# Making the sparse heads' masks beside the dilated heads instead of behind the threshold search

## The chip, the core and the metric

The kernel runs on one core of one Trainium2 chip. The core has five engines with a queue of instructions each, executed in order: TensorE (PE; its weight loads are shown apart as PEld), VectorE (DVE), ScalarE (ACT), GpSimd (POOL) and SyncE (SP), which issues the DMA transfers. The metric is the device time of one execution in microseconds (us).

## The reference

The reference is a decoder trunk of two layers on a sequence of 1024 tokens of 1024 numbers, all in float32. Each layer normalises x, projects it (`w_in`), runs 16 attention heads of three kinds, adds their output projection to x, and then runs a gated MLP with a short convolution. The three kinds of heads are:

- 4 MLA heads: causal attention with low-rank queries and keys;
- 8 dilated heads: the mixture of three dilated windows (1, 4 and 16), which the kernel computes as one attention with an additive mask `dil`;
- 4 sparse heads (DSA): an indexer scores every pair of query and key, and each query attends only its 256 best keys.

```
score = einsum(relu(q_idx . k_idx), w_idx)          # per query t and key s
score = where(s <= t, score, -inf)
_, sel = top_k(score, 256)                          # ties: the lower index wins
s = (q . k[sel]) * HEAD_DIM ** -0.5;  p = softmax(s);  o = p @ v[sel]
```

The kernel does not gather. For every query it finds the 256th best score (the threshold), and turns the score tile into an additive mask that is 0 for chosen keys and huge for the others.

## The kernel before, in words

Queries are cut into 8 blocks of 128, one per partition. The scores of block i, (i+1)*128 columns wide, lie in the tile `sc2` to `sc7`; blocks 0 and 1 have at most 256 keys and need no choice.

**The indexer** (`indexer`, L292 to L430) is a Python generator: it emits a few instructions, yields, and its caller emits other work in between. It makes the scores (up to L344), and then searches the thresholds bit by bit (L379 to L393): 32 rounds, in which VectorE counts for blocks 4, 5 and 6 (L365) and ScalarE for blocks 7, 3 and 2 (L384). **The masks** come last (L400 to L430). `select(i)` makes one: ScalarE takes the Sign of score minus threshold into a work tile (L405); VectorE marks the ties (L406), numbers them with a prefix sum (L407), works out how many ties are needed (L409, L410), and writes the mask over the score tile (L411, L412). Blocks 4, 5 and 6 come first. Then three steps count and look up the exact threshold of blocks 7, 3 and 2 (L417 to L426: count, mask off, minimum), L427 and L428 correct it, and these three blocks are selected. That is 15 yields: 6 for three blocks, 3 for the thresholds, 6 for three blocks. The work tiles have the tag `tk`, two slots of 4 KB.

**The order of the layer** (`layer`): the first projection (index queries and keys), the MLA projection with the MLA tiles, then six groups of 384 columns of the input projection (L745 to L769; matmul L285, eviction L754 and L756 into `zst`, from there by DMA to DRAM). Beside each tile of these the indexer is advanced by 6 yields (`step`, L760), and the MLA heads by 4 pieces. The weights of a column group lie in four tiles of the ring `w0` or `w1` (even or odd group), so the last group's lie in `w1`.

**The 12 dilated and sparse heads** (heads 4 to 11 dilated, 12 to 15 sparse; L828 to L844) follow as a software pipeline: in round h, the scores of head h+1 (`attn_scores`), the values of head h (`attn_values`) and the preparation of head h+2 (`attn_prep`) are woven together by `prop`, which advances each generator in proportion to its weight. The scores of a head take, for each block i, a matmul pair (L539), VectorE's evacuation with the mask and a running minimum (L541, 12 of them per head, tiles `pt0` to `pt7`), ScalarE's exponential (L545), a reciprocal (L547) and GpSimd's scaling (L549). The values take transposes of pt (L564), ScalarE's copy ph (L567), VectorE's remainder pl (L568) and matmuls (L572 to L575). Preparation is split on GpSimd (L203, L204, L522, L523), transposed (L501, L511) and copied by ScalarE (L502, L512). The mask of a sparse head is `sc[i]` (L808).

The tile framework gives each instruction a priority from its place in the program, raised by `high_priority`, and a scheduler lays down the order on each engine. So the order on an engine is not the program's, and the projection's last matmuls stand between the first heads' work.

**Memory** is laid out by hand. `LAY1` (projection stage) has `w1` at 80 to 104 KB and `tk` at 104 to 112; `LAY2` (heads 4 to 15) has head 5's `QA1` and `QB1` at 104 to 112, and nothing at 78 to 93.5. A tile waits for what last used its space.

Of the kernel before, what the change touches and what calls it, by code (L numbers as in the profile page):

```python
# [8 lines left out]
F32 = mybir.dt.float32  # L9
# [6 lines left out]
ALU = mybir.AluOpType  # L16

DEPTH = 2
S = 1024
D = 1024  # L20
P = 128
# [4 lines left out]
NEG = -3.0e38  # L26
TOPK = 256
# [10 lines left out]
PTS = [[(f"pt{i}{e}", 1, (i + 1) / 2) for i in range(8)] for e in range(2)]  # L38
# [5 lines left out]
LAYM = [(0, ("QA0", 1, 4), ("QB0", 1, 4), ("KS0", 1, 4), ("otmp", 1, 2), PTS[0][0], PTS[0][1], PTS[0][2], PTS[0][3], ("caus", 1, 4),  # L44
        ("VS", 1, 4), PTS[0][4], PTS[0][5], PTS[0][6], PTS[0][7], ("ph", 2, 2), ("pl", 2, 2), ("mix", 2, 2), ("KL", 1, 4))]
LAY2 = [(0, ("QA0", 1, 4), ("QB0", 1, 4), ("KS0", 1, 4), ("kx", 1, 4), ("qx", 1, 4), ("dil", 1, 4), ("VS", 2, 4), ("ph", 3, 2),
        ("pl", 3, 2), ("otmp", 1, 2), PTS[1][0], PTS[1][1], PTS[1][2], PTS[1][3], ("mix", 2, 2)), (56, PTS[0][7], PTS[0][1],
        PTS[0][2], PTS[0][3], PTS[0][4], PTS[0][6], PTS[0][0], ("KS1", 1, 4), PTS[0][5]), (93.5, PTS[1][5], PTS[1][6], PTS[1][7],
        ("QA1", 1, 4), ("QB1", 1, 4), ("VS", 1, 4), PTS[1][4], ("caus", 1, 1))]
at2 = lambda tag, *places: [(o, (tag, 1, 2)) for o in places]  # L50
# [89 lines left out]
class Trunk:  # L140
# [151 lines left out]
    def indexer(self, zi, sc, pool, causal_diag):  # L292

        nc = self.nc
# [31 lines left out]
        for h in range(8):  # L326
            qi, qn = qn, qprep(h + 1) if h < 7 else None
            yield
            for i in range(2, NT):
                wd = (i + 1) * P  # L330
# [20 lines left out]
        va, ve = ACT_TK, tuple(i for i in range(2, NT) if i not in ACT_TK)  # L351
# [5 lines left out]
        cv, ca, fa, na_ = cc[:, :nv], cc[:, nv:], ff[:, nv:], nn[:, nv:]  # L357
# [6 lines left out]
        def count(src, junk, out, thr, op):  # L364
            nc.vector.tensor_scalar(junk, src, thr, None, op0=op, op1=ALU.add, accum_out=out)  # L365

        cut, o, pack = {}, 2048, None
        for i in (*ve, None):
            wd = (i + 1) * P if i else (max(ve) + 1) * P
# [8 lines left out]
        for bit in range(31, -1, -1):  # L378
            w = -1.0 if bit == 31 else float(1 << bit)  # L379
            nxt = 1 << (bit - 1) if bit else 0  # L380
            for c in range(max(na, nv)):
                if c < na:
                    junk = self.main.tile([P, S], I8, name="junka", tag="junka", bufs=1)
                    nc.scalar.activation(junk[:, :(va[c] + 1) * P], sc[va[c]], AF.Sign, bias=ca[:, c:c + 1].bitcast(F32),  # L384
                                         accum_out=na_[:, c:c + 1])
# [9 lines left out]
        thr = {i: cv[:, c:c + 1].bitcast(F32) for c, i in enumerate(ve)}  # L395

        need, up = st("need", NT, F32), st("up", na, F32)
        nt_ = self.small.tile([P, NT, 8], F32, name="nt", tag="wi", bufs=1)[:, 0]

        def select(i):  # L400
            wd = (i + 1) * P
            sg, e = (pool.tile([P, S], F32, name="tk", tag="tk") for _ in range(2))
            sg, e, nd = sg[:, :wd], e[:, :wd], need[:, i:i + 1]
            nc.vector.tensor_scalar(nt_[:, i:i + 1], thr[i], -1.0, None, op0=ALU.mult)
            nc.scalar.activation(sg, sc[i], AF.Sign, bias=nt_[:, i:i + 1], accum_out=nd)  # L405
            nc.vector.tensor_scalar(e, sg, 0.0, None, op0=ALU.is_equal)  # L406
            nc.vector.tensor_tensor_scan(e, self.one.to_broadcast([P, wd]), e, 0.0, op0=ALU.mult, op1=ALU.add)  # L407
            yield
            nc.vector.tensor_scalar(nd, nd, -0.5, TOPK - wd / 2, op0=ALU.mult, op1=ALU.add)  # L409
            nc.vector.scalar_tensor_tensor(nd, e[:, wd - 1:wd], 0.5, nd, op0=ALU.mult, op1=ALU.add)  # L410
            nc.vector.scalar_tensor_tensor(e, e, nd, sg, op0=ALU.is_gt, op1=ALU.subtract)  # L411
            nc.vector.tensor_scalar(sc[i], e, 0.0, -NEG, op0=ALU.is_gt, op1=ALU.mult)  # L412
            yield

        for i in ve:
            yield from select(i)
        for c, i in enumerate(va):  # L417
            wd = (i + 1) * P
            t_ = ca[:, c:c + 1].bitcast(F32)
            b = pool.tile([P, S], F32, name="tk", tag="tk")  # L420
            count(sc[i], b[:, :wd], na_[:, c:c + 1], t_, ALU.is_gt)
            nc.vector.tensor_scalar(b[:, :wd], sc[i], t_, -NEG, op0=ALU.is_le, op1=ALU.mult)
            nc.vector.tensor_tensor_reduce(b[:, :wd], b[:, :wd], sc[i], op0=ALU.add, op1=ALU.min, scale=1.0,
                                           scalar=-NEG, accum_out=up[:, c:c + 1])
            thr[i] = t_
            yield  # L426
        nc.vector.tensor_scalar(fa, na_, float(TOPK), None, op0=ALU.is_ge)  # L427
        nc.vector.copy_predicated(ca.bitcast(F32), fa, up)  # L428
        for i in va:
            yield from select(i)  # L430

    def mla_tile(self, t, ps, kpe, up, pool, outs):

# [153 lines left out]
    def layer(self, l, hT):  # L587
        nc, tc, a = self.nc, self.tc, self.a
# [9 lines left out]
        sc = {i: scv.tile([P, (i + 1) * P], F32, tag=f"sc{i}") for i in range(2, NT)}  # L598
        pool = View(tc, 56, LAYS[0][0], *LAY1)
# [94 lines left out]
        def prop(*gens):  # L694

            st = [[0.0, 1.0 / m, g_] for m, g_ in gens]
            while st:
                e = min(st, key=lambda e_: e_[0] + e_[1] / 2)
                if next(e[2], 0) == 0:
                    st.remove(e)  # L700
                else:
                    yield
                e[0] += e[1]
# [18 lines left out]
        def fin(kb, mix):  # L722
            kg, kk = divmod(kb, 4)
            for g in range(2):
                hi = self.hT_tile(mixh, g, kg, 0)[:, kk]
                lo = self.hT_tile(mixh, g, kg, 1)[:, kk]
                self.split(hi, lo, mix[g], FE[g], "pool")
# [51 lines left out]
        pool = View(tc, 80, LAYS[0][0], *LAY2)  # L779
# [37 lines left out]
        def chain(*items):  # L817
            items = [i for i in items if i]
            def gen():
                for i in items:  # L820
                    yield from i[1]
            return (sum(i[0] for i in items), gen()) if items else None

        SC = lambda h, g: (4, self.attn_scores(heads[h], g, pool)) if h < n else None
        VA = lambda h, g: (4 * g + 5, self.attn_values(heads[h], g, pool)) if 0 <= h < n else None
        PR = lambda h: chain((5, self.attn_prep(heads[h], pool)), (1, self.attn_prep_v(heads[h], pool))) if h < n else None

        def go(*items):  # L828
            for _ in prop(*[i for i in items if i]):
                pass  # L830
        with tc.high_priority(HP2):
            go(PR(4))
            go(chain(SC(4, 0), SC(4, 1)), PR(5))
        for h in range(4, n):
            if h == SW:
                self.banks(**B2)
            if h in FIN:
                kb = FIN.index(h)
                z = self.main.tile([P, 2, 512], F32, name="zm", tag="raw", bufs=3)
                nc.sync.dma_start(z, mD[:, kb])  # L840
                fin(kb, (z[:, 0], z[:, 1]))
            with tc.high_priority(HP2 if h <= HPH else 0):
                go(chain(SC(h + 1, 0), SC(h + 1, 1)), chain(VA(h, 0), VA(h, 1)), PR(h + 2))
        pool.close()  # L844
        scv.close()
        return mixh
# [369 lines left out]
```

## Time and profile before

| | |
|---|---|
| median of the runs shown (3) | 2788.01 us (2786.67 to 2792.11) |
| the profiled execution's own time | 2787.77 us |
| its span, first to last instruction | 2786.0 us |
| mean granted TensorE clock | 0.991 of full speed |
| TensorE busy | 2671.8 us (96%) |
| VectorE busy | 2265.9 us (81%) |

The profile's page gives the busy time of each engine, the costliest groups of instructions by line and the chain of work that ended last; the trace behind it answers by window, line or tile. A matmul's end is modelled, so a busy TensorE is not necessarily at its peak. Layer 0 lies in the first half of the span, layer 1 in the second, with the same stages.

### The profile page before, as it was taken

What the parts mean: (1) busy time and instruction counts of PE and PEld (TensorE: products, weight loads), DVE (VectorE), ACT (ScalarE), POOL (GpSimd) and SP (SyncE); (2) the same over time, 40 slices, a digit from 0 to 9 for tenths busy, and PEclk for the clock granted to TensorE, in tenths of its full rate; (3) what the DMA queues carried; (4) which work ended last, traced back from release to release, by engine and by line L of the source; (5) the groups of instructions that cost most, each with busy time, mean ns of one, the idle gap of its engine ahead of it and who ended that gap; (6) DMA issues with size and microseconds to landing.
All of it is one profiled execution on the core that took longest, in us unless ns stands there. A gap on an engine that the chain in (4) does not pass through costs nothing.

```text
span 2786.0 us, 40647 instructions
## 1 busy us (share of the span) xinstructions
PE 2671.8 (96%) x13576; PEld 2264.1 (81%) x13576; DVE 2265.9 (81%) x4347; ACT 1564.8 (56%) x3414; POOL 1728.5 (62%) x1910
## 2 busy tenths in 40 slices
PE   7999999999899999999999999999998999999997
PEld 7898988878787787777789989888787777877775
DVE  7779996874788888889867799788648888888887
ACT  4567857982444454454445778489624444444443
POOL 5364467971576677777534445689517677767764
PEclk9999999999999999999999999999999999999999
DMA  5322323341111111211333223233501111111111
GB/s 166 101 90 87 101 82 90 99 132 45 38 46 51 52 50 50 63 55 46 99 100 108 88 77 108 85 95 92 160 9 38 54 46 54 60 49 51 54 53 76
DMA packets 224013, 208.85 MB, mean 75 GB/s; under 512 B 21852, under 2 KB 197820, under 8 KB 223804
## 3 DMA queue, kind: packets, MB, share of 16 engines
q1 hardware_dynamic: 223804, 206.26, 24.5%
q8 instruction: 107, 1.75, 0.3%
q14 instruction: 102, 0.84, 0.1%
HBM read 153.80 MB, written 39.85 MB: 70 GB/s over the span
## 4 chain that ended last, share of the span: by engine, by line
PE 68%; DVE 15%; POOL 6%; issue 5%; ACT 4%; DMA 3%; SPq 0%; POOLq 0%; ACTq 0%; DVEq 0%
PE psum L969 23%; PE psum L285 11%; PE psum L1071 10%; PE psum L934 6%; PE psum L539 4%; PE psum L564 4%; DVE cut L365 2%; DVE psum L1030 2%; DVE x L1075 2%; PE psum L575 2%; PE psum L574 1%; PE psum L572 1%; PE psum L1127 1%; POOL wu L204 1%; PE psum L335 1%
## 5 line engine op out<-in xcount | busy, mean ns | idle before, releaser
L204 POOL TENSOR_TENSOR wu<-raw,wu 128x256 fp32r<-128x256 f32 x584 | 480.2, 841 | 316.5 <-ACT wu L199 311.7
L285 PE MATMUL psum<-wi,hT 128*128 128x384 f32 (+1 forms) x3072 | 603.1, 339 | 0.9 <-ACT zst L756 0.9
L285 PEld LDWEIGHTS psum<-wi,hT 128*128 128x128 f32 x3072 | 528.8, 190 | 10.9 <-ACT zst L756 1.3
L969 PE MATMUL psum<-hT,wu 128*128 128x512 f32 x1824 | 491.2, 400 | 19.0 <-ACT wu L199 10.0
L1071 PE MATMUL psum<-wd,act 128*128 128x512 f32 x1680 | 470.3, 396 | 21.1 <-DVE x L1075 12.4
L199 ACT ACTIVATE wu<-raw 128x256 fp32r<-128x256 f32 x584 | 232.0, 415 | 439.8 <-PE psum L969 300.2
L1075 DVE TENSOR_TENSOR x<-psum,x 128x512 f32<-128x512 f32 x640 | 419.0, 682 | 37.2 <-PE psum L1071 36.7
L969 PEld LDWEIGHTS psum<-hT,wu 128*128 128x128 f32 x1824 | 346.1, 190 | 106.5 <-ACT wu L199 11.7
L1071 PEld LDWEIGHTS psum<-wd,act 128*128 128x128 f32 x1680 | 313.4, 188 | 107.1 <-DVE x L1075 22.4
L969 PE MATMUL psum<-T,wu 128*128 128x512 f32 x1440 | 380.7, 395 | 2.5 <-ACT act L199 1.3
L969 PEld LDWEIGHTS psum<-T,wu 128*128 128x128 f32 x1440 | 268.9, 188 | 70.5 <-POOL wu L204 3.3
L549 POOL TENSOR_SCALAR pt<-pt,rl 128x128 f32<-128x128 f32 (+7 forms) x256 | 192.0, 765 | 133.6 <-DVE rl L547 103.0
L568 DVE TENSOR_TENSOR pl<-psum,ph 128x512 fp32r<-128x512 f32 (+3 forms) x384 | 206.2, 552 | 37.7 <-ACT ph L567 35.6
L545 ACT ACTIVATE pt<-pt,nm 128x128 f32<-128x128 f32 (+7 forms) x256 | 198.7, 777 | 47.2 <-DVE nm L541 45.0
L204 POOL TENSOR_TENSOR act<-yu,act 128x512 fp32r<-128x512 f32 x140 | 195.9, 1399 | 43.4 <-ACT act L199 41.7
L204 POOL TENSOR_TENSOR wd<-wr,wd 128x512 fp32r<-128x512 f32 x140 | 197.5, 1411 | 9.0 <-ACT wd L199 8.6
L564 PE MATMUL psum<-ident,pt 128*128 128x128 f32 x1152 | 193.1, 276 | 9.6 <-DVE QB L514 4.5
L192 POOL TENSOR_TENSOR rs<-ms,mhalf 128x1 f32<-128x1 f32 (+1 forms) x56 | 37.5, 670 | 252.1 <-DVE ms L189 249.4
L567 ACT ACTIVATE ph<-psum 128x512 fp32r<-128x512 f32 (+3 forms) x384 | 179.0, 487 | 22.5 <-PE psum L564 17.5
L934 PE MATMUL psum<-wo,hT 128*128 128x512 f32 x768 | 190.5, 404 | 0.0
L384 ACT ACTIVATE junka<-sc,cc 128x1024 int8<-128x1024 f32 (+2 forms) x192 | 158.5, 825 | 40.1 <-DVE cc L393 32.1
L564 PEld LDWEIGHTS psum<-ident,pt 128*128 128x128 f32 x1152 | 141.1, 141 | 39.9 <-POOL pt L549 7.5
(234 smaller groups left out, 5309.6 us busy)
## 6 DMA issues: line engine op xcount, KB each, us to landing
raw<-in_w_up_dram SPq DMA_DIRECT2D x88, 512.0 KB, 4.0
raw<-in_w_in_dram SPq DMA_DIRECT2D x56, 384.0 KB, 3.4
wr<-in_w_down_dram SPq DMA_DIRECT2D x40, 512.0 KB, 3.3
z<-zst SPq DMA_DIRECT2D x96, 192.0 KB, 1.9
z<-z SPq DMA_DIRECT2D x36, 512.0 KB, 4.6
QB<-KS SPq DMA_DIRECT2D x96, 128.0 KB, 2.3
x<-in_x_dram SPq DMA_DIRECT2D x16, 512.0 KB, 5.1
raw<-in_w_o_dram SPq DMA_DIRECT2D x16, 512.0 KB, 3.4
```

The source lines that it names most:

```text
L199: nc.scalar.activation(hi, src, AF.Copy)
L204: (nc.vector if le == "dve" else nc.gpsimd).tensor_tensor(lo, src, r32(hi), op=ALU.subtract)
L285: mm = nc.tensor.matmul(ps[:, :w], l_, r_, start=(n == 0), stop=(n == 3 * KD - 1))
L545: nc.scalar.activation(pt, pt, AF.Exp, bias=nm, scale=-1.0, accum_out=ls[:, i % 2:i % 2 + 1])
L549: nc.gpsimd.tensor_scalar(p_, p_, rl[:, e:e + 1], 0.0, op0=ALU.mult, op1=ALU.add)
L564: nc.tensor.transpose(ps[:, (i - 4 * g) * P:(i - 4 * g + 1) * P], Pt[i][:, j * P:(j + 1) * P], self.ident)
L567: nc.scalar.activation(ph[:, off:], ps[:, off:], AF.Copy)
L568: nc.vector.tensor_tensor(pl[:, off:], ps[:, off:], r32(ph[:, off:]), op=ALU.subtract)
L934: nc.tensor.matmul(ps, l_, r_, start=(i == 0), stop=(i == 3 * KD - 1))
L969: nc.tensor.matmul(ps, l_, r_, start=(start and i == 0), stop=(stop and i == 11), skip_group_check=resume)
L1071: nc.tensor.matmul(ps, l_[:, a_, t * P:(t + 1) * P], r_[:, b_], start=(start and i == 0), stop=i == 2, skip_group_check=not start)
L1075: nc.vector.tensor_tensor(xs, ps, xs, op=ALU.add)
```

## The change

The masks' part of the indexer becomes a generator of its own, `masks(pool)`, which the indexer only defines. The layer starts it with the pool of the head stage, where two `tk` slots are added at 81 to 89 KB, and weaves it into rounds 4 to 8 of the heads, three yields in each: 5 x 3 = 15, all of it. What each instruction computes is unchanged.

```
-LAY2 = [(0, ...), (56, PTS[0][7], PTS[0][1],
+LAY2 = [(0, ...), (81, ("tk", 2, 4)), (56, PTS[0][7], PTS[0][1],
...
-        def select(i):
+        def select(i, pool):
...
-        for i in ve:
-            yield from select(i)
-        for c, i in enumerate(va):
...
-        for i in va:
-            yield from select(i)
+        def masks(pool):
+            for i in ve:
+                yield from select(i, pool)
+            for c, i in enumerate(va):
...
+            for i in va:
+                yield from select(i, pool)
+
+        self.masks = masks
...
+        masks = self.masks(pool)
+
+        def part(gen, m):
+            for _ in range(m):
+                next(gen, None)
+                yield
...
-                go(chain(SC(h + 1, 0), SC(h + 1, 1)), chain(VA(h, 0), VA(h, 1)), PR(h + 2))
+                go(chain(SC(h + 1, 0), SC(h + 1, 1)), chain(VA(h, 0), VA(h, 1)), PR(h + 2),
+                   (3, part(masks, 3)) if 4 <= h < 9 else None)
```

Lines behind L414 are renumbered in the kernel after: by 4 in the rest of the indexer and in the heads' functions (L541 becomes L545, L568 becomes L572), by 12 behind the heads' loop.

On VectorE, right behind the last round of the search in layer 0, the masks of blocks 4 and 5 (score tiles `sc_119` and `sc_120`) follow in the kernel before:

```order
L404 TENSOR_SCALAR nt<-cc 128x1
L568 TENSOR_TENSOR pl<-psum,ph 128x128
L409 TENSOR_SCALAR need<-need 128x1
L406 TENSOR_SCALAR tk<-tk 128x640
L407 SCALAR_TENSOR_TENSOR tk<-one,tk 128x640
L410 SCALAR_TENSOR_TENSOR need<-tk,need 128x1
L411 SCALAR_TENSOR_TENSOR tk<-tk,need 128x640
L412 TENSOR_SCALAR sc_119<-tk 128x640
L582 TENSOR_TENSOR mix<-psum,otmp 64x512
L409 TENSOR_SCALAR need<-need 128x1
L406 TENSOR_SCALAR tk<-tk 128x768
```

At the same place in the kernel after, the first scores of head 4 stand (L545 is the old L541; `pt_5055` and the next are its first key rows):

```order
L404 TENSOR_SCALAR nt<-cc 128x1 x3
L394 TENSOR_SCALAR cc<-cc 128x3
L572 TENSOR_TENSOR pl<-psum,ph 128x128
L586 TENSOR_TENSOR mix<-psum,otmp 64x512
L545 ISA pt_5055,nm<-psum,dil 128x128
L545 ISA nm 128x1
L545 ISA pt_5072,nm<-psum,dil 128x256
```

Nothing of the masks but the negated thresholds is left there. The second place on VectorE is head 5's fifth key row (`pt_5375` before, `pt_5317` after), which follows the projection's last matmuls. Before:

```order
L568 TENSOR_TENSOR pl<-psum,ph 128x384
L568 TENSOR_TENSOR pl<-psum,ph 128x256
L568 TENSOR_TENSOR pl<-psum,ph 128x128
L541 ISA pt_5375,nm<-psum,dil 128x512
L541 ISA nm 128x1
L541 ISA pt_5375,nm<-psum,dil,nm 128x128
L541 ISA nm 128x1
L541 ISA pt_5414,nm<-psum,dil 128x512
```

After, with what each instruction waits for besides its own engine's order:

```order
L406 TENSOR_SCALAR tk<-tk 128x640 [waits PE_49]
L572 TENSOR_TENSOR pl<-psum,ph 128x512 [waits Activation_49]
L407 SCALAR_TENSOR_TENSOR tk<-one,tk 128x640 [waits DVE_49]
L572 TENSOR_TENSOR pl<-psum,ph 128x384 [waits PE_49,Activation_49]
L410 SCALAR_TENSOR_TENSOR need<-tk,need 128x1 [waits DVE_49]
L411 SCALAR_TENSOR_TENSOR tk<-tk,need 128x640 [waits DVE_49]
L572 TENSOR_TENSOR pl<-psum,ph 128x512 [waits Activation_49]
L412 TENSOR_SCALAR sc_119<-tk 128x640 [waits DVE_49]
L545 ISA pt_5317,nm<-psum,dil 128x512 [waits DMAHW4_49,DMAHW2_49,DMAHW5_49,DMAHW1_49,DMAHW7_49,DMAHW0_49,Pool_49]
L545 ISA nm 128x1
L409 TENSOR_SCALAR need<-need 128x1 [waits Activation_49]
L406 TENSOR_SCALAR tk<-tk 128x768 [waits DVE_49]
```

The masks have moved in between the heads' evacuations and remainders, from here to head 9's seventh key row in layer 0 and to just behind head 10's first in layer 1, and their first step waits for TensorE. On ScalarE the Signs have moved with them. Here the first two of them are seen among the evacuations ph (L571, the old L567) of the values and head 5's exponential (L549, the old L545):

```order
L405 ACTIVATE tk,need<-sc_119,nt 128x640 [waits PE_49]
L571 ACTIVATE ph<-psum 128x512 [waits DVE_49,PE_49] x2
L760 ACTIVATE zst<-psum 128x384 [waits DMAHW0_49,PE_49,Pool_49]
L571 ACTIVATE ph<-psum 128x384 [waits DVE_49,PE_49]
L571 ACTIVATE ph<-psum 128x512 [waits PE_49]
L516 ACTIVATE QA<-psum 128x512 [waits DVE_49,PE_49]
L405 ACTIVATE tk,need<-sc_120,nt 128x768 [waits DVE_49]
L571 ACTIVATE ph<-psum 128x128 [waits DVE_49,PE_49]
L571 ACTIVATE ph<-psum 128x256 [waits PE_49]
L549 ACTIVATE pt_5317,ls<-pt_5317,nm 128x640 [waits DMAHW0_49,DMAHW7_49,DVE_49,Pool_49]
```

The second Sign waits for VectorE, since the two work slots are shared by all masks.

More of the change, by code (lines that the diff above doesn't have):

```diff
@@ L46 @@
 LAY2 = [(0, ("QA0", 1, 4), ("QB0", 1, 4), ("KS0", 1, 4), ("kx", 1, 4), ("qx", 1, 4), ("dil", 1, 4), ("VS", 2, 4), ("ph", 3, 2),
-        ("pl", 3, 2), ("otmp", 1, 2), PTS[1][0], PTS[1][1], PTS[1][2], PTS[1][3], ("mix", 2, 2)), (56, PTS[0][7], PTS[0][1],
+        ("pl", 3, 2), ("otmp", 1, 2), PTS[1][0], PTS[1][1], PTS[1][2], PTS[1][3], ("mix", 2, 2)), (81, ("tk", 2, 4)), (56, PTS[0][7], PTS[0][1],
         PTS[0][2], PTS[0][3], PTS[0][4], PTS[0][6], PTS[0][0], ("KS1", 1, 4), PTS[0][5]), (93.5, PTS[1][5], PTS[1][6], PTS[1][7],
@@ L413, in select @@
             yield
-        for i in ve:
-            yield from select(i)
-        for c, i in enumerate(va):
[L418 to L428, printed above, removed]
-        for i in va:
-            yield from select(i)
+        def masks(pool):
+            for i in ve:
+                yield from select(i, pool)
+            for c, i in enumerate(va):
+                wd = (i + 1) * P
+                t_ = ca[:, c:c + 1].bitcast(F32)
+                b = pool.tile([P, S], F32, name="tk", tag="tk")
+                count(sc[i], b[:, :wd], na_[:, c:c + 1], t_, ALU.is_gt)
+                nc.vector.tensor_scalar(b[:, :wd], sc[i], t_, -NEG, op0=ALU.is_le, op1=ALU.mult)
+                nc.vector.tensor_tensor_reduce(b[:, :wd], b[:, :wd], sc[i], op0=ALU.add, op1=ALU.min, scale=1.0,
+                                               scalar=-NEG, accum_out=up[:, c:c + 1])
+                thr[i] = t_
+                yield
+            nc.vector.tensor_scalar(fa, na_, float(TOPK), None, op0=ALU.is_ge)
+            nc.vector.copy_predicated(ca.bitcast(F32), fa, up)
+            for i in va:
+                yield from select(i, pool)
+        self.masks = masks
     def mla_tile(self, t, ps, kpe, up, pool, outs):
@@ L826, in layer @@
         PR = lambda h: chain((5, self.attn_prep(heads[h], pool)), (1, self.attn_prep_v(heads[h], pool))) if h < n else None
+        masks = self.masks(pool)
+        def part(gen, m):
+            for _ in range(m):
+                next(gen, None)
+                yield
         def go(*items):
```

## Prediction

> **What bounds the kernel now.** I read the page first, then cut the two layers into stretches with the table of windows, then looked up the masks in the groups by line, and last the order of time around them. The page says that TensorE is the busiest engine over the whole run, so a stretch in which it works without a break cannot be shortened by moving VectorE's work.
>
> ```profile
> span 2786.0 us, 40647 instructions
> PE 2671.8 (96%) x13576; PEld 2264.1 (81%) x13576; DVE 2265.9 (81%) x4347; ACT 1564.8 (56%) x3414; POOL 1728.5 (62%) x1910
> ```
>
> The shares are means over stages with different limits. Four instants cut layer 0: the search for the thresholds ends at about 374 us, the last matmul of the input projection (L285) starts at 437.55, head 5 makes its fifth key row (L541, pt4) at 444.88, and head 9 makes its seventh (pt6, counted as the 69th score evacuation of the dilated heads) at 503.30.
>
> ```profile
> 437.55 0.42 PE L285 MATMUL psum<-wi,hT 128*128 128x384 f32 x1
> ...
> 444.88 0.69 DVE L541 CUSTOM_DVE_ANT_0 pt<-psum,dil 128x512 f32<-128x512 f32 x1 [2.32 <-DMA z<-zst]
> ...
> 503.30 0.68 DVE L541 CUSTOM_DVE_ANT_0 pt<-psum,dil 128x512 f32<-128x512 f32 x1
> ```
>
> The windows between them (columns: length, then busy time and instructions of PE, weight load, DVE, ACT, POOL, then granted clock and DMA):
>
> ```profile
> core 0: us, PE busy (x) PEld busy (x) DVE busy (x) ACT busy (x) POOL busy (x), PEclk, DMA share, GB/s
> 374.00:437.60 63.60, 57.69 (x351) 53.81 (x349) 49.32 (x112) 28.84 (x67) 39.62 (x61) 1.00 0.31 90
> 437.60:444.90 7.30, 5.57 (x37) 4.43 (x35) 2.79 (x7) 4.00 (x9) 7.05 (x12) 1.00 0.51 135
> 444.90:503.30 58.40, 56.72 (x365) 48.01 (x366) 49.75 (x162) 53.02 (x127) 48.55 (x59) 0.97 0.35 92
> 503.30:624.00 120.70, 117.25 (x766) 99.73 (x766) 101.11 (x287) 107.59 (x246) 102.59 (x114) 0.99 0.40 114
> ```
>
> Two different regimes stand here. In the first window the projection's matmuls fill TensorE, which is busy 57.69 of 63.60 us, and the masks run on VectorE beside them: TensorE loses at most 63.60 - 57.69 = 5.9 us, whatever causes it. In the third window every engine is nearly full: VectorE 49.75 of 58.40 us (85%), ScalarE 91%, GpSimd 83%, TensorE 97%. VectorE has 58.40 - 49.75 = 8.65 us to spare there. This is where the change puts the masks.
>
> Layer 1 has the same shape. Its windows are cut at the same instructions, except that its last mask falls later in the new order, behind head 10's first row, so the third window ends there:
>
> ```profile
> 1754.00:1815.70 61.70, 57.14 (x340) 53.96 (x339) 46.59 (x97) 27.39 (x64) 44.31 (x64) 0.97 0.33 95
> 1820.20:1885.30 65.10, 64.55 (x437) 55.55 (x436) 58.36 (x183) 60.93 (x145) 56.52 (x69) 1.00 0.32 84
> 1885.30:1997.60 112.30, 109.23 (x719) 93.19 (x719) 92.70 (x270) 100.44 (x231) 96.00 (x107) 1.00 0.42 119
> ```
>
> **What is moved, and what it costs.** The groups of VectorE between 373 and 420 us hold the whole of layer 0's masks; the eight costliest of them (columns: count, busy us and mean ns, then idle time ahead) are these.
>
> ```profile
> L407 DVE TENSOR_TENSOR_SCAN tk<-one,tk 128x640 f32<-128x640 f32 (+5 forms) x6 | 10.9, 1811 | 0.1
> L411 DVE SCALAR_TENSOR_TENSOR tk<-tk,need 128x640 f32<-128x640 f32 (+5 forms) x6 | 6.2, 1041 | 0.2
> L412 DVE TENSOR_SCALAR sc<-tk 128x640 f32<-128x640 f32 (+5 forms) x6 | 4.9, 820 | 0.1
> L406 DVE TENSOR_SCALAR tk<-tk 128x640 f32<-128x640 f32 (+5 forms) x6 | 3.8, 625 | 0.1
> L423 DVE CUSTOM_DVE_ANT_0 tk<-tk,sc 128x1024 f32<-128x1024 f32 (+2 forms) x3 | 2.9, 979 | 0.0
> L422 DVE TENSOR_SCALAR tk<-sc,cc 128x1024 f32<-128x1024 f32 (+2 forms) x3 | 2.6, 881 | 0.0
> L365 DVE TENSOR_SCALAR_CACHE_REDUCE tk<-sc,cc 128x1024 f32<-128x1024 f32 (+2 forms) x3 | 2.6, 871 | 0.0
> L410 DVE SCALAR_TENSOR_TENSOR need<-tk,need 128x1 f32<-128x1 f32 x6 | 2.0, 328 | 0.2
> ```
>
> They sum to 35.9 us in a layer. The rest of the step is six Signs on ScalarE (L405) and a few very short instructions; no DMA, no matmul and nothing on GpSimd belongs to it, so no DMA queue is moved past anything. No instruction is added or taken away: the total work stays, and only its place counts.
>
> Term 1, the head start. With the masks gone from the first window, the heads' short chains no longer queue behind them, and TensorE can close its idle time there: between 0 and 5.9 us in layer 0, and 61.70 - 57.14 = 4.6 us in layer 1. About as many TensorE instructions stand ahead of the last projection matmul in the new order as in the old (a difference of some ten in 2400), so the projection's end comes earlier by that idle time and by no more. I take all of it, -5.9 and -4.6, because what TensorE waits for there is late GpSimd and VectorE work.
>
> Term 2, the first tile. The masks now need two work slots that lie in the projection's weight ring, so their first VectorE step waits for the projection's end, and so do the parts pl of head 4's values, which stand behind it in VectorE's queue and for which TensorE waits. That falls into the 7.30 us of the second window, where VectorE is busy for 2.79 and waits for the write of a `zst` tile (2.32 us in the row at 444.88), because head 5's pt4 takes over that space. The tile of 640 columns costs there what it costs now:
>
> ```profile
> 375.46 0.48 DVE L406 TENSOR_SCALAR tk<-tk 128x640 f32<-128x640 f32 x1
> 375.98 1.78 DVE L407 TENSOR_TENSOR_SCAN tk<-one,tk 128x640 f32<-128x640 f32 x1
> 377.79 1.07 DVE L410 SCALAR_TENSOR_TENSOR need<-tk,need 128x1 f32<-128x1 f32 x1
> 378.90 0.88 DVE L411 SCALAR_TENSOR_TENSOR tk<-tk,need 128x640 f32<-128x640 f32 x1
> 379.82 0.49 DVE L412 TENSOR_SCALAR sc<-tk 128x640 f32<-128x640 f32 x1
> ```
>
> That is 4.7 us, against 7.30 - 2.79 = 4.5 us idle: nothing on the path. If that cover is gone because the write lands sooner, it costs its 4.7 us.
>
> Term 3, the other five tiles and the three count-and-minimum steps: 35.9 - 4.7 = 31.2 us of VectorE, between the same instructions that now take 58.40 us. VectorE then owes 49.75 + 31.2 = 80.95 us, and it executes in order, so the stretch cannot be shorter than that. How dense VectorE gets when it is the bound shows around the search's end, where search and masks keep it busy for 47.32 of 50 us:
>
> ```profile
> 350.00:400.00 50.00, 45.79 (x278) 43.49 (x277) 47.32 (x103) 28.31 (x72) 32.39 (x50) 1.00 0.29 88
> ```
>
> Between 95% (this row) and 100% I take 97.5%, as many short independent instructions stand between the masks' steps: 80.95 / 0.975 = 83.0 us, or +24.6. In layer 1 it is (58.36 + 31.2) / 0.975 = 91.9 against 65.10, or +26.8. What is late next is the rows pt and the parts pl, so TensorE waits for VectorE in the middle of the dilated heads, where no projection matmul is left to fill in.
>
> Term 4, what comes after. Behind the last mask the old cadence returns. Heads run ahead by one at most in the code, and TensorE is busy for 117.25 of 120.70 us and 109.23 of 112.30, so at most 3.45 + 3.07 = 6.5 us could be given back; I take 0.
>
> The sum: 24.6 - 5.9 + 26.8 - 4.6 = +40.9 us on the profiled execution's own 2787.77 us (span 2786.0), which is 0.24 us from the median of the runs shown, 2788.01. Forecast: 2828 us.
>
> Bounds of term 3. GpSimd and VectorE get in each other's way when both work on SBUF:
>
> ```profile
> 381.13 0.55 DVE L406 TENSOR_SCALAR tk<-tk 128x768 f32<-128x768 f32 x1
> 383.90 0.39 POOL L217 TENSOR_TENSOR rope_b<-zst,rt 128x96 f32<-128x96 f32 x1
> 385.14 1.51 DVE L412 TENSOR_SCALAR sc<-tk 128x768 f32<-128x768 f32 x1
> 387.56 2.10 DVE L407 TENSOR_TENSOR_SCAN tk<-one,tk 128x896 f32<-128x896 f32 x1
> 387.74 2.10 POOL L217 TENSOR_TENSOR rope_b<-zst,rt 128x96 f32<-128x96 f32 x1
> ```
>
> The same small rope step of GpSimd takes 0.39 us, and 2.10 when it starts inside a scan, ending as the scan ends; L412 takes 1.51 us beside a GpSimd instruction where the like L406 of the same width took 0.55. I read some 5 us of such waiting out of the 35.9 (L410's mean of 328 ns for one column, L412's mean above L406's, say). In the third window GpSimd is busier, 83% against 62%, so the masks may cost 5 us a layer more than now; without any waiting they would cost 5 less. Low end: (80.95 - 5) - 58.40 - 5.9 and (89.56 - 5) - 65.10 - 4.6 give +26.5 us, 2814; with 6.5 given back, 2808. High end: 5 us more, 95% density and no head start give +32.1 and +34.4, 2854.
>
> The Trainium skill, page "SBUF — State Buffer", section "SBUF: two separate sides", says that VectorE and GpSimd share a pair of ports as an exclusive lock: an instruction of VectorE with two SBUF inputs or in a two-port mode, and one of GpSimd, block each other for their whole length. The rope rows of this trace agree with that rule (2.10 us against 0.39). It speaks against this change, as the masks leave a stage where GpSimd is busy for 62% for one with 83%; by it the sum would lie nearer the high end than the low.
>
> **The rivals.** A: the masks vanish in idle time. Then only term 1 is left, -10.5 us, 2777 us. For it speaks that VectorE is below 90% in every dilated window; against it that the spare time is 8.65 and 65.10 - 58.36 = 6.7 us, and 31 are asked for. It decides only if the masks' VectorE time in the stretch fell below those. B: waits multiply. A Sign (L405) must wait until VectorE is done with the tile before, and behind it in ScalarE's queue now stand the evacuations ph and the exponentials that feed VectorE. Before, four such waits took 11.7 us and hurt nobody:
>
> ```profile
> L405 ACT ACTIVATE tk<-sc,nt 128x640 f32<-128x640 f32 (+5 forms) x6 | 5.3, 883 | 14.0 <-DVE tk L411 11.7 <-DVE nt L404 2.3
> ```
>
> ScalarE is busy for 53.02 of 58.40 us where they go. If they recur at that size and VectorE starves for half of them, 6 us a layer come on top, 2840; together with the port waits and a lower density it is the high end, 2854. C: the loss is made up, since the later heads are ordered better and TensorE can go below its modelled busy time (its weight loads are busy only 99.73 of 120.70 us). If half of term 3 came back, 0.5 x 51.4 = 25.7 us, the time would be 2803. D: the change doing nothing is out, since the new order has the masks among the heads on VectorE and ScalarE; no change could only come from C with all of term 3 less 10.5 us made up, 2788.
>
> **How the numbers follow.** The forecast has 0.60, B 0.20, C 0.09, A 0.06, and no change 0.05. The range leaves out A, no change and some of C: it takes in the bounds from just under the low end, 2804, to just over the high end, 2858. Faster by over 0.2% (some 5.6 us, about what a measurement of this kernel can tell): A, 0.06. Within 0.2%: 0.05. Slower: 0.89.
>
> **What would show it.** In the profile after, the first stretch, from the search's end to the last L285, should be shorter by 4 to 6 us with TensorE busy throughout and VectorE half idle; from head 5's pt4 to head 9's pt6 it should take some 83 us instead of 58.4, with VectorE at 95% or more and TensorE waiting for L541 and L568; from there to the end of the heads it should take 121 us as before. The forecast is wrong if VectorE stays under 90% in the middle stretch (B, if that stretch is long all the same), if the mask lines sum to under 25 us or over 42 in a layer, or if the window behind the masks falls below 117 us (C).

## The result and the profile after

The kernel after takes 2829.81 us (median of 4 runs, 2823.49 to 2834.25), the kernel before 2788.41 us (4 runs on the same chip, 2786.67 to 2792.11). The ratio is 1.0149, with a 95% interval of 1.0134 to 1.0165: 41.4 us slower. The profiled execution of the kernel after has a span of 2827.0 us, 41.0 more than before, so its rows can be set against those of before. Of all runs in this document one, of the kernel woven into seven rounds, took 9507 us, and medians and ratios leave it out.

The page of the kernel after, its span and the busy time of each engine:

```profile
span 2827.0 us, 40635 instructions
PE 2698.1 (95%) x13576; PEld 2277.9 (81%) x13576; DVE 2257.3 (80%) x4347; ACT 1566.9 (55%) x3414; POOL 1719.5 (61%) x1910
```

VectorE did no more work than before (2257.3 us against 2265.9). Over the whole run nothing points at the loss; it has to be looked for by stretch. The timeline of the kernel after has the same three instants in layer 0: the last rows of L285, head 5's fifth key row and head 9's seventh.

```profile
428.87 1.98 PE L285 MATMUL psum<-wi,hT 128*128 128x384 f32 x10
...
435.23 0.68 DVE L545 CUSTOM_DVE_ANT_0 pt<-psum,dil 128x512 f32<-128x512 f32 x1
...
518.89 0.69 DVE L545 CUSTOM_DVE_ANT_0 pt<-psum,dil 128x512 f32<-128x512 f32 x1 [0.18 <-PE psum L543]
```

The table of windows of the kernel after, cut at those instants (columns as in the prediction): layer 0, then the last three windows of layer 1, where the last rows of L285 end at 1837.44, and then the middle stretch of layer 0 cut once more behind its last mask:

```profile
core 0: us, PE busy (x) PEld busy (x) DVE busy (x) ACT busy (x) POOL busy (x), PEclk, DMA share, GB/s
374.00:430.90 56.90, 56.90 (x356) 54.78 (x355) 15.24 (x51) 25.29 (x58) 29.39 (x62) 1.00 0.40 114
430.90:435.20 4.30, 2.97 (x17) 2.15 (x16) 4.26 (x7) 3.26 (x7) 3.52 (x7) 1.00 0.13 46
435.20:518.90 83.70, 71.56 (x386) 56.13 (x384) 80.49 (x220) 59.97 (x139) 57.58 (x61) 0.86 0.23 59
518.90:641.00 122.10, 115.44 (x758) 98.99 (x757) 100.29 (x283) 106.62 (x244) 104.81 (x116) 0.99 0.40 117
...
1837.44:1842.35 4.91, 3.87 (x19) 2.47 (x18) 4.24 (x8) 2.98 (x6) 4.08 (x7) 1.00 0.11 40
1842.35:1929.70 87.35, 75.25 (x425) 58.61 (x426) 85.13 (x231) 64.98 (x153) 63.96 (x68) 0.90 0.24 63
1929.70:2043.80 114.10, 109.68 (x720) 93.17 (x719) 94.10 (x270) 101.01 (x231) 96.74 (x108) 1.00 0.42 117
...
435.20:505.50 70.30, 58.16 (x304) 44.68 (x302) 68.85 (x182) 48.16 (x110) 49.79 (x50) 0.85 0.24 62
505.50:518.90 13.40, 13.40 (x84) 11.45 (x83) 11.64 (x40) 11.82 (x29) 7.79 (x11) 0.91 0.18 40
```

The prediction cut the first window of before where the last row of L285 starts; here it is cut where that row ends, which in the kernel before is 437.55 + 0.42 = 437.97. From the search's end (374.19 us before, 373.91 after) to that end, layer 0's first stretch goes from 63.8 to 56.9 us (-6.8), the gap behind it from 6.9 to 4.4 (-2.5), the middle stretch from 58.4 to 83.7 (+25.3), and the rest from 120.7 to 122.1 (+1.4). In the middle stretch VectorE is busy for 80.49 of 83.70 us (96%), TensorE for only 71.56; in layer 1 VectorE for 85.13 of 87.35 (97%). As long as masks stand in the stretch, up to 505.5 us, VectorE is busy for 98% of it, and for 87% behind them. In the first stretch TensorE has no idle time left, and VectorE is down from 49.32 to 15.24 us.

The waits inside the middle stretch (columns: total us, times, longest), first of the kernel before, from 444.9 to 503.3 us:

```profile
PEld psum L539 <- DVE nm L541: 4.2, 5, 2.4
PE psum L539 <- DVE nm L541: 2.8, 2, 2.2
```

and then of the kernel after, from 435.2 to 518.9 us (L543 and L545 are the old L539 and L541):

```profile
POOL pt L553 <- DVE rl L551: 19.5, 6, 4.5
PEld psum L543 <- DVE nm L545: 10.0, 11, 2.1
ACT pt L549 <- DVE nm L545: 8.6, 6, 2.6
...
PE psum L543 <- DVE nm L545: 7.0, 7, 1.8
DVE pt L545 <- PE psum L543: 2.5, 5, 0.9
```

All three other engines now wait for VectorE: TensorE's score matmuls for its score evacuations, ScalarE's exponentials for the same rows, GpSimd's scaling for its reciprocals. VectorE itself waits for TensorE for only 2.5 us.

### The profile page after: what moved, and what is told of

The parts are those of the page before. It is cut to its first block, busy times and chain, and to the rows that moved or that the text cites. A ratio compares the mean times of both kernels' runs of the same rounds, so it can differ in the third digit from the quotient of the medians.

```text
span 2827.0 us, 40635 instructions
## 1 busy us (share of the span) xinstructions
PE 2698.1 (95%) x13576; PEld 2277.9 (81%) x13576; DVE 2257.3 (80%) x4347; ACT 1566.9 (55%) x3414; POOL 1719.5 (61%) x1910
## 4 chain that ended last, share of the span: by engine, by line
PE 71%; DVE 16%; issue 4%; ACT 3%; POOL 3%; DMA 2%; SPq 0%; POOLq 0%; ACTq 0%; DVEq 0%
PE psum L981 24%; PE psum L285 13%; PE psum L1083 11%; PE psum L946 6%; PE psum L543 4%; PE psum L568 3%; DVE psum L1042 2%; DVE x L1087 2%; PE psum L579 2%; DVE cut L365 1%; DVE pt L545 1%; PE psum L578 1%; PE psum L1139 1%; PE psum L576 1%; PE psum L241 1%
## 5 line engine op out<-in xcount | busy, mean ns | idle before, releaser
L285 PE MATMUL psum<-wi,hT 128*128 128x384 f32 (+1 forms) x3072 | 607.4, 340 | 1.2 <-ACT zst L758 0.8
L285 PEld LDWEIGHTS psum<-wi,hT 128*128 128x128 f32 x3072 | 530.6, 191 | 11.6 <-ACT zst L758 1.7
L572 DVE TENSOR_TENSOR pl<-psum,ph 128x512 fp32r<-128x512 f32 (+3 forms) x384 | 206.5, 550 | 26.9 <-ACT ph L571 24.9
L549 ACT ACTIVATE pt<-pt,nm 128x128 f32<-128x128 f32 (+7 forms) x256 | 198.0, 775 | 53.4 <-DVE nm L545 46.4
L568 PE MATMUL psum<-ident,pt 128*128 128x128 f32 x1152 | 199.4, 281 | 10.0 <-DVE QB L518 3.1
L571 ACT ACTIVATE ph<-psum 128x512 fp32r<-128x512 f32 (+3 forms) x384 | 178.8, 487 | 51.2 <-PE psum L568 44.9
L568 PEld LDWEIGHTS psum<-ident,pt 128*128 128x128 f32 x1152 | 144.7, 144 | 43.2 <-POOL pt L553 5.8
```

The source lines that it names most:

```text
L285: mm = nc.tensor.matmul(ps[:, :w], l_, r_, start=(n == 0), stop=(n == 3 * KD - 1))
L549: nc.scalar.activation(pt, pt, AF.Exp, bias=nm, scale=-1.0, accum_out=ls[:, i % 2:i % 2 + 1])
L568: nc.tensor.transpose(ps[:, (i - 4 * g) * P:(i - 4 * g + 1) * P], Pt[i][:, j * P:(j + 1) * P], self.ident)
L571: nc.scalar.activation(ph[:, off:], ps[:, off:], AF.Copy)
L572: nc.vector.tensor_tensor(pl[:, off:], ps[:, off:], r32(ph[:, off:]), op=ALU.subtract)
```

## The experiments

Each kernel was timed beside the kernel before on the same chip. The last column of the table is made from the profiled executions: the time from the last step of the search (L394) to the last value of the heads (L582, or L586 in the new numbering), both layers added, less that of before. It leaves out the stages that no kernel touches. For the kernel before it is (623.31 - 374.19) + (1996.85 - 1749.95) = 496.0 us, for the kernel after (640.25 - 373.91) + (2043.09 - 1777.29) = 532.1.

| kernel | median us | ratio to before, 95% interval | heads, us against before |
|---|---|---|---|
| after | 2829.81 | 1.0134 to 1.0165 | +36.1 |
| before, without the masks | 2778.17 | 0.9941 to 0.9974 | -12.1 |
| after, without the masks | 2777.34 | 0.9938 to 0.9970 | -12.2 |
| after, counts in place of four steps | 2821.20 | 1.0084 to 1.0152 | +29.6 |
| after, without the prefix sum | 2811.11 | 1.0059 to 1.0100 | +19.1 |
| after, three work slots | 2830.51 | 1.0136 to 1.0182 | +40.7 |
| after, woven into seven rounds | 2822.65 | 1.0097 to 1.0151 | +29.4 |
| three masks early, three woven | 2799.16 | 1.0024 to 1.0051 | +10.9 |
| before, last step on ScalarE | 2781.71 | 0.9965 to 0.9990 | -9.7 |
| after, last step on ScalarE | 2820.73 | 1.0092 to 1.0132 | +32.1 |

**What do the masks cost in either place?** The theory says that they cost VectorE's time only where VectorE sets the pace. Two kernels leave the masks out. One is the kernel before, with a return ahead of the masks:

```diff
+        return
         for i in ve:
             yield from select(i)
```

> The kernel before with all of the masks' step left out (the sparse heads add the raw scores as a mask, so the output is not the reference's). Theory (VectorE's time counts only where the other engines are full): beside the projection the masks cost only the idle time of TensorE there, 5.9 + 4.6 us, so 2778 us. Rival (the masks were hidden altogether before): 2788. Rival (they delay the heads by all of their VectorE time there too): 2720.

The other is the kernel after, without the third item of the weave:

```diff
-                   (3, part(masks, 3)) if 4 <= h < 9 else None)
+                   None)
```

> The kernel after with the masks' generator never advanced: same leaving out as in the run above, but the layout and the weaving of the kernel after. Theory: it is VectorE's 31 us a layer in the full stretch that cost the time, so without them 2778 us, like the run above, 52 us below the kernel after, and the stretch from head 5's fifth key row to head 9's seventh is 58 us again. Rival (the new layout or the new order of the heads costs by itself): it stays above 2795.

They took 2778.17 and 2777.34 us. So the masks cost 2789.71 - 2778.17 = 11.5 us for both layers in their old place (the kernel before, timed beside them, took 2789.71), and 2829.81 - 2777.34 = 52.5 in the new one, for the same instructions. The windows of the kernel after without masks show why: its projection stretch, its middle stretch, and the middle stretch of layer 1.

```profile
374.00:433.01 59.01, 59.01 (x369) 56.88 (x368) 16.41 (x62) 24.56 (x58) 30.65 (x66) 1.00 0.39 111
...
436.59:493.60 57.01, 55.88 (x358) 46.05 (x358) 48.33 (x161) 52.39 (x126) 49.97 (x61) 1.00 0.34 90
...
1812.55:1875.14 62.59, 61.44 (x397) 50.90 (x398) 53.32 (x174) 57.47 (x136) 55.42 (x68) 1.00 0.36 96
```

Beside the projection TensorE is busy throughout without masks as with them moved away, so what they cost there is TensorE's idle time of before and the gap behind it. In the middle stretch of layer 0 VectorE has 57.01 - 48.33 = 8.7 us to spare. With masks it has 80.49 - 48.33 = 32.2 us more to do, uses up those 8.7 but for 83.70 - 80.49 = 3.2, and the rest is the loss: 32.2 - 8.7 + 3.2 = 26.7 = 83.70 - 57.01. In layer 1 it is 31.8 - 9.3 + 2.2 = 24.7.

**Is it VectorE's time, or its quarrel with GpSimd over SBUF?** In the kernel after, the four steps L406, L407, L411 and L412 were replaced by four counts of the score tile, of the same width:

```diff
-            nc.vector.tensor_scalar(e, sg, 0.0, None, op0=ALU.is_equal)
-            nc.vector.tensor_tensor_scan(e, ...)
+            for _ in range(2):
+                count(sc[i], e, nd, thr[i], ALU.is_ge)
...
-            nc.vector.scalar_tensor_tensor(e, e, nd, sg, op0=ALU.is_gt, op1=ALU.subtract)
-            nc.vector.tensor_scalar(sc[i], e, 0.0, -NEG, op0=ALU.is_gt, op1=ALU.mult)
+            for _ in range(2):
+                count(sc[i], sg, nd, thr[i], ALU.is_ge)
```

> The kernel after, in which the four wide VectorE steps of each mask (L406, L407, L411, L412) are replaced by four counts of the score tile (the form of L365: one SBUF input, no second port); the masks are not written. VectorE's time falls from the 26.4 us that these four lines take in the kernel after to some 22 a layer, and the waits between VectorE and GpSimd go. Theory (VectorE's time is the cost): some 4 us a layer less, 2821 us. Rival (the waits of VectorE and GpSimd for each other are the cost): more than half of the loss goes, below 2810.

In another, only the prefix sum (L407) was left out:

```diff
-            nc.vector.tensor_tensor_scan(e, self.one.to_broadcast([P, wd]), e, 0.0, op0=ALU.mult, op1=ALU.add)
```

> The kernel after with the prefix sum of the ties (L407, 10.2 us a layer) left out, so ties at the threshold are not broken by index. Theory: 10.2 / 0.975 a layer, 2809 us. Rival (port waits: the scans are the longest instructions that shut GpSimd out): GpSimd's lost time comes back on top, below 2800. Rival (Signs at the head of ScalarE's queue are the cost): they come only 1.7 us earlier each, above 2815.

They took 2821.20 and 2811.11 us, both as the theory had it; the second saves 18.7 us for 10.2 us of prefix sums in layer 0 and 9.7 in layer 1. With the counts the last mask reaches beyond head 9's seventh key row (515.41 us). The window to head 10's first row takes in nearly all of it:

```profile
437.26:524.24 86.98, 72.54 (x430) 54.96 (x431) 86.14 (x252) 65.95 (x153) 61.56 (x72) 0.99 0.29 78
```

VectorE is busy for 99% of it; the same window takes 88.98 us in the kernel after. That the quarrel exists, the groups of GpSimd show, here the step that splits the keys, in the middle stretch before and after:

```profile
L204 POOL TENSOR_TENSOR kx<-z,kx 128x512 fp32r<-128x512 f32 x4 | 5.1, 1287 | 0.3
...
L204 POOL TENSOR_TENSOR kx<-z,kx 128x512 fp32r<-128x512 f32 x4 | 7.2, 1797 | 0.0
```

With the counts the split of the keys took 1302 again:

```profile
L204 POOL TENSOR_TENSOR kx<-z,kx 128x512 fp32r<-128x512 f32 x4 | 5.2, 1302 | 0.1
```

By the rule of the Trainium skill that the prediction weighed (page "SBUF — State Buffer", section "SBUF: two separate sides"), a step of VectorE with two SBUF inputs or in a two-port mode and a step of GpSimd block each other, and the longer GpSimd steps agree with it. But GpSimd waits for VectorE for 19.5 us of the stretch, which is room for its longer steps, and the counts saved 8.6 us in two layers, give or take some 10: what the theory gives for their shorter time, and not the 20 of the rival. They do not free VectorE of the whole quarrel, since L410 stays, which reads two tiles of SBUF for one column. In that run one L410 of layer 0 took 3.55 us, while GpSimd worked through three steps of its splits, and it ended as the last of these ended, at 520.82 us:

```profile
517.05 2.55 POOL L204 TENSOR_TENSOR hT<-zm,hT 128x512 fp32r<-128x512 f32 x2
517.28 3.55 DVE L410 SCALAR_TENSOR_TENSOR need<-tk,need 128x1 f32<-128x1 f32 x1
519.52 1.30 POOL L204 TENSOR_TENSOR hT<-mix,hT 128x512 fp32r<-128x512 f32 x1
```

So a part of VectorE's busy time looks like waiting for GpSimd. The prediction put it at some 5 us a layer in the old place. How much it is in the new place no run here shows, but the sum of the mask steps hardly grew (below).

**Do the Signs hold up ScalarE?** A third work slot lets a Sign start before VectorE is done with the tile ahead:

```diff
-LAY2 = [(0, ...), (81, ("tk", 2, 4)), ...
+LAY2 = [(0, ...), (79, ("tk", 3, 4)), ...
```

> The kernel after with three work slots for the masks instead of two, so that a Sign need not wait for VectorE to be done with the tile before. Theory (VectorE's time is the cost): within 4 us of the kernel after, 2826 to 2834. Rival (Signs that wait at the head of ScalarE's queue hold up the evacuations behind them): some 6 us a layer less, 2818 or below.

It took 2830.51 us: no change. The profile of the kernel after says so as well: from 428 us on ScalarE is idle for 0.6 us ahead of its five remaining Signs, where the six of before waited for 14.0.

```profile
L405 ACT ACTIVATE tk<-sc,nt 128x768 f32<-128x768 f32 (+4 forms) x5 | 4.4, 890 | 0.6 <-DVE tk L411 0.6
```

The third slot did move work: VectorE got further with the masks ahead of head 5's fifth key row. In layer 0 VectorE is busy for 8.71 of the 8.74 us of the gap ahead of that row, and for 71.12 of the 74.43 us of the middle stretch. The middle stretch is 9.3 us shorter than in the kernel after and the gap 4.4 longer, and the heads as a whole came out no faster (+40.7 us in the table).

**Does it help to spread the masks thinner?** Seven rounds in place of five:

```diff
-                   (3, part(masks, 3)) if 4 <= h < 9 else None)
+                   (2, part(masks, 3 if h == 4 else 2)) if 4 <= h < 11 else None)
```

> The kernel after with the same masks woven into seven rounds of heads (4 to 10) instead of five, two or three pieces in each. Theory: two more rounds lend their idle VectorE time, 8.65 us for four heads, so some 4 us a layer: 2821 us. Rival (each mask costs its time wherever it stands among the full heads): 2830. Rival (thin pieces fit into gaps, dense ones do not): half of the loss goes, 2810.

It took 2822.65 us, near the theory's 2821, but with an interval (some 2815 to 2830 us) that holds the first rival too. The edit also did less than it says: the scheduler put the last mask's L412 at 510.5 us in place of 504.3. This one settles nothing.

**Does the cost grow with the work that is moved?** The masks of blocks 4, 5 and 6 were left behind the search, and the rest woven in, two yields a round:

```diff
+        for i in ve:
+            yield from select(i, pool)
         def masks(pool):
-            for i in ve:
-                yield from select(i, pool)
...
-                   (3, part(masks, 3)) if 4 <= h < 9 else None)
+                   (2, part(masks, 2)) if 4 <= h < 9 else None)
```

> The masks of blocks 4, 5 and 6 stay behind the search, beside the projection; only the threshold steps and masks of blocks 7, 3 and 2 are woven into rounds 4 to 8. Theory: the early three fall into VectorE time that is idle (13 us ahead of head 4's first scores); of the late 21 us some 4.5 fit into the wait for the last zst writes and 8.65 or 6.7 into idle time, the head start stays: 4 to 5 us a layer over the kernel before, 2797 us. Rival (any VectorE work late costs in full): 2815. Rival (the early masks alone cost the head start): 2807.

It took 2799.16 us, as the theory had it: moving the part of three blocks with their thresholds costs 11 us, and moving all of it 41. In layer 0 the threshold steps ran ahead of the middle stretch (the last of them at 443.31 us), and the three masks in its first 29.4 us. The window of the stretch, and the same cut behind the last mask:

```profile
444.58:510.83 66.25, 59.60 (x373) 48.91 (x374) 61.53 (x187) 56.38 (x135) 54.18 (x62) 0.97 0.31 82
444.58:474.00 29.42, 22.95 (x123) 17.10 (x124) 29.02 (x83) 21.64 (x49) 19.94 (x20) 0.94 0.25 67
474.00:510.83 36.83, 36.65 (x252) 31.82 (x251) 32.51 (x104) 34.74 (x88) 34.24 (x42) 1.00 0.35 94
```

VectorE is busy for 93% of the stretch, but for 99% of it beside the masks and 88% behind them. The stretch keeps 66.25 - 61.53 = 4.7 us of idle VectorE time and is still 9.2 us longer than without masks (57.01). So the spare time that counts is that of the part in which the masks stand, not that of the whole stretch.

**Can VectorE be relieved?** The mask's last step was written by ScalarE, as a Relu with a huge scale, in the kernel before and in the kernel after:

```diff
-            nc.vector.tensor_scalar(sc[i], e, 0.0, -NEG, op0=ALU.is_gt, op1=ALU.mult)
+            nc.scalar.activation(sc[i], e, AF.Relu, scale=1.0e38)
```

> The kernel before, with the last step of each mask (L412, the mask written over the scores, 4.9 us of VectorE in a layer) on ScalarE, as a Relu with a factor of 1e38 (the mask is then 1e38 or 2e38 in place of 3e38). Beside the projection ScalarE is busy for 28.84 of 63.6 us. Theory: VectorE is freed of 4.9 us there and the port it shares with GpSimd of six instructions, so 1 to 3 us of the 10.5 come back: 2786 us. Rival (Signs and evacuations queue behind the new step on ScalarE): 2789 or above.

> The kernel after, with the mask's last step (line 412, 4.6 us of VectorE in the middle stretch of layer 0) written by ScalarE instead of VectorE; the same work, on an engine that is 60 us busy of 83.7 there. Theory, VectorE's work sets the length of the stretch: it gets shorter by 4.6 / 0.96 = 4.8 us in each layer, so 2829.8 - 9.6 = 2820, and VectorE stays busy 95% or more of it. Rival, the stretch is set by the round trips between VectorE and ScalarE (a wait in ScalarE's queue ahead of the exps): one more step that waits there makes it no shorter, 2828 to 2836. If GpSimd's wait for the port were what matters, the result would be at or under 2815.

In the kernel after it gave 2820.73 us, which is what the theory gave. The profile bears that out only in part. Its middle stretch is 1.8 us shorter in layer 0, not 4.8, and 1.7 in layer 1. The window of layer 0:

```profile
439.89:521.77 81.88, 67.27 (x386) 51.71 (x384) 78.81 (x212) 63.00 (x147) 59.97 (x62) 0.94 0.24 62
```

VectorE is still busy for 96% of both (in layer 1 for 81.78 of 85.61 us), and got rid of less than 4.6 us, because other mask steps got longer there: L424 and L425 took 758 and 814 ns in the kernel after, and here 1202 and 1222.

The heads of its profiled execution are 532.1 - 528.1 = 4.0 us shorter; where the other 5 of its median lie is open. How long a mask step takes depends on what it happens to meet: L412 took 0.43 us for 512 columns and 1.19 for 384 in layer 0 of the kernel after.

In the kernel before the same edit gave 2781.71 us, 6.5 less than the 2788.21 of the kernel before beside it: faster than both kernels, and more gain than was expected. The windows show its projection stretch, the gap behind, and its middle stretch:

```profile
374.00:435.99 61.99, 57.16 (x335) 53.59 (x334) 45.74 (x107) 31.73 (x71) 40.09 (x60) 0.97 0.31 92
435.99:439.73 3.74, 3.74 (x28) 3.19 (x27) 1.30 (x3) 2.57 (x5) 3.00 (x8) 1.00 0.15 53
439.73:499.65 59.92, 59.74 (x405) 51.48 (x405) 53.29 (x171) 56.08 (x136) 52.62 (x64) 1.00 0.39 103
```

TensorE's idle time beside the projection is 61.99 - 57.16 = 4.8 us against 5.9. The gap behind it is 3.7 us against 6.9, the largest gain of layer 0; the middle stretch is 1.5 us longer than before and the rest of the layer's heads 2.9 shorter (117.75 us), which was not followed up. The order of the transfers accounts for most of the gap's change, as far as the traces show; no run changed that order alone. SyncE's queue in the kernel before, from 438 to 441 us:

```profile
438.02 1.11 SPq L507 DMA_DIRECT2D QB<-KS  x2
439.46 0.56 SPq L788 DMA_DIRECT2D z<-z  x1
440.37 0.36 SPq L759 DMA_DIRECT2D z<-zst  x1
```

and in the kernel before with the last step on ScalarE:

```profile
437.61 0.32 SPq L759 DMA_DIRECT2D z<-zst  x1
438.62 1.11 SPq L507 DMA_DIRECT2D QB<-KS  x2
```

The write of `zst`, for which head 5's fifth row waits, stands behind two copies of head 5's keys and a load of 512 KB in the one, and ahead of them in the other. In the kernel after, the copies and the load went out at 414.63 and 420.96 us, beside the projection, and the write at 433.24 had the queue to itself. From the issue of the write to that row it took 444.88 - 440.37 = 4.5 us in the kernel before, 439.73 - 437.61 = 2.1 with the last step on ScalarE, and 435.23 - 433.24 = 2.0 in the kernel after.

## Why the prediction was right, point by point

- **Term 1, the head start**, was -5.9 and -4.6 us. The trace has -6.8 in layer 0, and in layer 1 the time from the search's last step to the end of the last projection matmul went from 65.7 to 60.1 us, -5.6. TensorE is busy for the whole of the first stretch, as foretold. "By that idle time and by no more" was wrong by 1 us in each layer, the time by which TensorE is busy for less ahead of that point than before (56.9 us against 57.9 in layer 0). Without masks TensorE is busy throughout there as well.
- **Term 2, the first tile free in the gap**, was 0. The tile did fall into the gap, and VectorE is busy for 4.26 of its 4.30 us. The gap of before, in layer 0 and in layer 1, by the same cut:

```profile
437.97:444.88 6.91, 5.20 (x34) 4.20 (x33) 2.47 (x6) 3.63 (x9) 6.67 (x12) 1.00 0.54 142
1815.69:1820.20 4.51, 4.47 (x32) 3.70 (x31) 1.38 (x2) 2.67 (x5) 2.77 (x6) 1.00 0.64 186
```

In layer 0 the gap shrank by 2.5 us. The step that failed there is "no DMA queue is moved past anything": no transfer belongs to the masks, but with the heads' chains running earlier, head 5's copies and a load left the queue ahead of the `zst` write. In layer 1, for which the prediction did not work this term out, the gap of before had only 3.1 us of idle VectorE time for a tile of some 4.7, and it grew by 0.4 us.
- **Term 3, the middle stretch**, was +24.6 and +26.8 us; it measured +25.3 and +22.25. The rule, VectorE's time over a density between 95% and 100%, held (96% and 97%, against the 97.5% taken). In layer 1 the term was too large by 4.6 us. It started from VectorE's 58.36 us of before; the kernel without masks has only 53.32 in the same stretch, in 174 VectorE instructions instead of 183. So with the head start a part of the heads' work falls ahead of the stretch, and 53.32 with the prediction's own 31.2 us of masks makes 84.5, near the 85.13 of the kernel after. In layer 0 the difference was small (48.33 against 49.75).
- **The bounds of term 3**, 5 us of waiting for GpSimd either way: the eight groups of mask steps of layer 0 moved the waiting about and nearly kept their sum, 37.0 us against 35.9. They read in the kernel after:

```profile
L407 DVE TENSOR_TENSOR_SCAN tk<-one,tk 128x640 f32<-128x640 f32 (+5 forms) x6 | 10.2, 1697 | 0.0
L411 DVE SCALAR_TENSOR_TENSOR tk<-tk,need 128x640 f32<-128x640 f32 (+5 forms) x6 | 7.7, 1275 | 0.1
L412 DVE TENSOR_SCALAR sc<-tk 128x640 f32<-128x640 f32 (+5 forms) x6 | 4.6, 760 | 0.0
L406 DVE TENSOR_SCALAR tk<-tk 128x640 f32<-128x640 f32 (+5 forms) x6 | 3.9, 648 | 0.0
L410 DVE SCALAR_TENSOR_TENSOR need<-tk,need 128x1 f32<-128x1 f32 x6 | 3.3, 554 | 0.0
L365 DVE TENSOR_SCALAR_CACHE_REDUCE tk<-sc,cc 128x1024 f32<-128x1024 f32 (+2 forms) x3 | 2.6, 866 | 0.0
L425 DVE CUSTOM_DVE_ANT_0 tk<-tk,sc 128x1024 f32<-128x1024 f32 (+2 forms) x3 | 2.4, 814 | 0.0
L424 DVE TENSOR_SCALAR tk<-sc,cc 128x1024 f32<-128x1024 f32 (+2 forms) x3 | 2.3, 758 | 0.0
```

L411 and L410 are longer than before (1041 and 328 ns), L407 shorter (1811). The masks did not get dearer by 5 us. GpSimd is busy for 57.58 of 83.70 us (69%) of the slower stretch and not for the 83% that the prediction took over from before; that this is the reason was not tested.
- **Term 4, what comes after**, was 0 and measured +1.4 and +1.8: nothing is given back.
- The sum of these is -12.4 - 2.1 + 47.5 + 3.2 = +36.2 us, as the table has it (+36.1), against the +40.9 forecast and the 41.0 by which the spans differ. The last 5 us lie in stages that the change doesn't touch. The one between layer 0's heads and layer 1's search end took 1126.6 us in the profiled execution before and 1137.0 after (+10.4), and between 1127 and 1140 in those of the experiments, with no relation to the masks. What follows layer 1's heads took 789.1 and 783.9 us (-5.2). So the forecast's nearness to the median is partly luck: term 3 was 4 us too large, terms 1 and 2 gave 4 us more than was put down, term 4 cost 3, and the other stages happened to add 5.
- **Rival A**, masks that vanish, fell with the 52.5 us that they cost. **Rival B**, waits that multiply at the Signs, fell with the 0.6 us of the Signs' waits and with the third slot, which left the time as it was. **Rival C**, a loss made up later, fell with the window behind the masks, 122.1 us.

## What to carry to other kernels

Work that leaves an engine's idle time is paid by the spare time of the stretch it goes to, not by the mean of the run: here VectorE was 81% busy over the run, but had 9 us to spare where 32 were put, and gave back only the 11 us that the masks had cost in their old place. What counts is the spare time beside the moved work itself: three masks packed into 29 us cost 9 us there although VectorE had time left behind them. Read the spare time of both places from windows of the trace before moving anything, and from the trace without the work if one can be had, since the move also shifts other work into and out of the stretch. If an engine is to be relieved, another engine can take a step where the work stands; that won 6.5 us here, in part through the order of the transfers, where the move lost 41. The Trainium skill, page "Perfetto Trace Analysis", section "Optimizing Scalar/DVE Operations", advises that for a saturated VectorE; here it paid also in a stretch where VectorE was busy for 49.32 of 63.60 us.

## What the runs showed of the hardware

- The granted TensorE clock fell to 0.86 and 0.90 in the two middle stretches, from 0.97 and 1.00, while TensorE waited for VectorE. It isn't what made them long: with the counts in place of four steps the granted clock was 0.99 to head 10's first row, and that still took 86.98 us (88.98 in the kernel after), with VectorE busy for 86.14.
- TensorE's busy time can't be read as work there. It is 71.56 us for 386 matmul records in the middle stretch after, and 56.72 for 365 before. The records' ends are modelled; at the lower clock the 386 would take 56.72 / 365 x 386 x 0.97 / 0.86 = 67.7 us by an estimate from these rows, and what the other 4 us are the runs don't show.
- A step one column wide can take very different times: L410 took 554 ns in the mean in layer 0 of the kernel after and 295 in layer 1, and 3.55 us once in the run with the counts, beside three steps of GpSimd. What the others met was not followed up.
